# A hybrid attention and MoE block on one core: program order on TensorE from the output projection on, one weight load behind the last router scores, and a tail by token tiles

## The chip, the core and the metric

The kernel runs on one core of a Trainium2 chip. Its engines work side by side, each on its own queue of instructions in order: TensorE (PE, matmuls and transposes, with PEld for its weight loads), VectorE (DVE), ScalarE (ACT), GpSimd (POOL) and SyncE (SP), which here does nothing but issue transfers. They wait for each other by semaphores. The metric is the device time of one execution in microseconds (us), lower is better.

## What is computed

The block takes x of 512 tokens x 1024 columns. A condition vector gives shifts, scales and gates; two causal attention mixers run side by side, are gated and merged, and one output projection adds them to x. Then comes the part that this change is about:

```python
h = rms_norm(x, g_ffn_norm[l]) * (1.0 + scale_f) + shift_f
x = x + gate_f * moe_ffn(h, ...)
return rms_norm(x, g_final)

scores = sigmoid(xf @ w_router)                     # 512 x 64 experts
choice = scores + b_router
# the best 4 of 8 groups (by the sum of their top two), the top 6 experts in them
gate = take_along_axis(scores, expert_idx); gate = gate / gate.sum(-1) * 2.5
# every token goes to its 6 experts, rows sorted by expert
hb = silu(xb @ w_exp_gate[e]) * (xb @ w_exp_up[e])  # 1024 -> 256
routed += (hb @ w_exp_down[e]) * g[:, None]         # 256 -> 1024
shared = (silu(xf @ w_sh_gate) * (xf @ w_sh_up)) @ w_sh_down
```

There are 64 experts of 3 MB each in f32 and one shared expert of the same size. 512 x 6 rows are spread over them.

## The kernel before

All tokens stay on the core. Tokens are taken in four tiles of 128 (index i), the output projection also in four chunks of 256 columns (index c). A matmul is f32; where both factors are split in a high and a low part it is done in three passes (`mm3`, L155 to L158).

**From the output projection to the router.** `out_proj(i, c)` multiplies the merged mixers by a chunk of w_out and adds the gated result to `acc[:, i]`, the running x. When a token tile has all four chunks, `norm2(i)` (L902) normalises it: a sum of squares on ACT, a power on POOL, a scaled copy `h2p` on DVE, which is stored to `h2d` in DRAM for the later gathers and turned by eight PE transposes (`tp`) into `h2T`. `score(i)` (L919) multiplies `h2T` by the router weights into `lg` (L925), copies it to `lgT` on ACT and adds its halves by a second matmul (L929), and takes an exponential on ACT (`sc`). `route(i)` (L934) is a chain of small DVE operations that ends in `sel`, the 0/1 choice of experts for each token. `place(i)` (L981) counts with PE the rows ahead of each token (`pos`: `sel` of the earlier tiles by ones, of its own by a triangle) and makes addresses; `scatter(i)` (L998) writes six columns to a `table` in DRAM by indirect transfers of POOL. `shared_in` (L1013) is the first layer of the shared expert (`og` and `ou`, then `hs`), `shared_out` (L1028) the second (`so`, added to `acc` on DVE). From the counts of all four tiles (`cr`, `cc`) the kernel then ranks the experts by their load (`pm`, `sched`, L1050 to L1078) and finds those with more rows than their slots hold (`ob`, `om`, L1080 to L1115).

In this part a scheduler arranges PE's instructions of before by its own estimates; `follow` ties a few of them to others, and the table `SEQ` sets the order of the program's steps.

**The expert tiles.** Four experts are fixed ones, whose weights are loaded before the ranking is known; the others are loaded in order of rank, into six weight slots. The rows lie in 33 tiles of 128 rows, each with up to four experts. Per tile: `fetch` gathers 128 rows of `h2d` by an indirect POOL transfer into one of three buffers (two `xg` and the space of `hs`), `turn` transposes them (`tp`, `xT`), `first` multiplies by gate and up (`gu`), `hide` applies silu, `turn_hidden` transposes, `expert_out` multiplies by down (`y`), and `combine` adds the rows back to their tokens by matmuls with a one-hot `oht` (`o`, high and low part `yH`, `yL`). PE and SP are in an order written by hand (`manual_schedule`), and `ENTRY` is the order of the first transfers: g, u and d with a number are gate, up and down weights of a tile's first experts, s the pieces of the table, f a gather, e a reading of the ranking.

**The tail.** The last tile (number 32) multiplies in two groups of two experts; `seed` starts sums (`fo`) with `acc` by an identity matmul, y of the last tile is added to them, and when all four token tiles are done, ACT squares, POOL adds and takes powers, DVE scales, SP stores, one token tile after the other.

Of the kernel before, what the change touches and what calls it, by code (L numbers as in the profile page):

```python
# [10 lines left out]
F32 = mybir.dt.float32  # L11
# [6 lines left out]
ALU = mybir.AluOpType  # L18
# [21 lines left out]
HOLD = 0  # L40
HREST = (1, 2, 3)
FOL = 1
SEQ = (((2, 3), ()), ((3, 3), ["n0"]), ((2, 2), ()), ((3, 2), ["s0", "n1", "r0"]), ((2, 1), ()), ((3, 1), ["s1", "p0", "r1"]),
       ((2, 0), ()), ((3, 0), ["n2", "n3", "c0", "p1", "s2", "s3", "c1", "r2", "p2", "c2", "r3", "h0", "p3", "c3"]))
SEQ = [(p, [(t[0], int(t[1])) for t in todo]) for p, todo in SEQ]
PW = {0: 3, 1: 3}
CHM, SOB, SOC = 0, 2, 2
ENTRY = "e1 g1 s0 s1 f0 u1 s2 s3 f1 s4 s5 s6 s7 s8 d1 e3 g3 u3"
# [45 lines left out]
def build(ctx, tc, a, out, dbg=None):  # L94
# [593 lines left out]
    def load_expert(slot, e, parts=1, now=True):  # L688
# [126 lines left out]
    hs = keep.tile([128, 2, S], F32, name="hs")  # L815
    tb = keep.tile([128, TILES + 1, 2], I32, name="tb")
# [33 lines left out]
    scat = []  # L850

# [49 lines left out]
    def norm2(i):  # L901
        t = slice(i * 128, (i + 1) * 128)  # L902
        h2p = np2.tile([128, KD, 128], F32, name="h2p", bufs=2)
        A.activation(h2p.rearrange("p k f -> p (k f)"), acc[:, i], AF.Square, accum_out=st2[:, 0, i:i + 1])
# [4 lines left out]
        SP.dma_start(h2d[t], h2p.rearrange("p k f -> p (k f)"))  # L909
        for g in range(2):  # L910
            tp = tr_p.tile([128, S], F32, name="tp", tag="tr")
            for k in range(4):
                PE.transpose(tp[:, k * 128:(k + 1) * 128], h2p[:, g * 4 + k], ident)
# [6 lines left out]
    def score(i):  # L920
# [6 lines left out]
        A.copy(lgT, lg[:, :128])  # L927
        lg = mm_p.tile([128, S], F32, name="lg", tag="mm")
        PE.matmul(lg[:, :NE], lgT, pairs, start=True, stop=True)  # L929
        sc = rt.tile([128, NE], F32, name="sc", bufs=2)  # L930
        A.activation(sc, lg[:, :NE], AF.Exp, scale=-1.0)
        scores[i] = sc

    def route(i):  # L934
# [20 lines left out]
        chm = rt.tile([128, 8, 8], F32, name="chm")  # L955
        (V if CHM else G).memset(chm, NEG)
# [24 lines left out]
    def place(i):  # L981
        oh, ixf, pay = picks.pop(i)
        pos = mm_p.tile([128, S], F32, name="pos", tag="mm")
        for q in range(i):
            m = PE.matmul(pos[:, :NE], onesb, sel[:, q], start=(q == 0), stop=False)
            if q == 0 and FOL:
                follow(m, last[0])
        m = PE.matmul(pos[:, :NE], before, sel[:, i], start=(i == 0), stop=True)
        if FOL:
            follow(m, last[0])  # L990
# [22 lines left out]
    def shared_in(g, blocks=range(2)):  # L1013
        t = slice(g * 256, g * 256 + 256)
        for b in blocks:
            og = s_p.tile([128, S], F32, name="og", tag="s")
            ou = s_p.tile([128, S], F32, name="ou", tag="s")
            for j, o in ((0, og), (1, ou)):
                for k in range(KD):
                    m = PE.matmul(o[:, :256], wsg[:, j, k, b * 128:(b + 1) * 128], h2T[:, k, t],  # L1020
                                  start=(k == 0), stop=(k == KD - 1))
                    if k == 0 and g == 0 and 2 * b + j >= HOLD:
                        follow(m, last[0])
            A.activation(hs[:, b, t], og[:, :256], AF.Tanh, scale=0.5)
            V.scalar_tensor_tensor(hs[:, b, t], hs[:, b, t], 1.0, og[:, :256], op0=ALU.add, op1=ALU.mult)
            V.scalar_tensor_tensor(hs[:, b, t], hs[:, b, t], 0.5, ou[:, :256], op0=ALU.mult, op1=ALU.mult)

    def shared_out(rows):  # L1028
        for i in rows:
            for n in range(2):  # L1030
                o = mo_p.tile([128, S], F32, name="so", tag="y")
                for b in range(2):
                    PE.matmul(o, hs[:, b, i * 128:(i + 1) * 128], wsd[:, b, n * 512:(n + 1) * 512],
                              start=(b == 0), stop=(b == 1))
                c = slice(n * 512, n * 512 + 512)
                V.tensor_tensor(acc[:, i, c], acc[:, i, c], o, ALU.add)

    for c in range(4):
        for i in range(2):
            out_proj(i, c, chunks[c])  # L1040
# [17 lines left out]
    cr = mm_p.tile([128, S], F32, name="cr", tag="mm")  # L1058
    cc = mm_p.tile([128, S], F32, name="cc", tag="mm")
# [5 lines left out]
    rowk = rt.tile([128, NE], F32, name="rowk")  # L1065
# [3 lines left out]
    cmpk = rt.tile([NE, NE], F32, name="cmpk")  # L1069
    V.scalar_tensor_tensor(cmpk, rowk[0:NE], cnt[:, 1:2], ones[0:NE, 0:NE], op0=ALU.is_gt, op1=ALU.mult,  # L1070
                           accum_out=cnt[:, 2:3])
    ohr = rt.tile([NE, NE], F32, name="ohr")
    V.tensor_scalar(ohr, iota_e[0:NE], cnt[:, 2:3], None, op0=ALU.is_equal)
    pm = mm_p.tile([128, S], F32, name="pm", tag="mm")
# [3 lines left out]
    V.tensor_scalar(sched[:, 1], pm[0:1, :NE], float(STRIDE), None, op0=ALU.mult)  # L1078

# [396 lines left out]
```

## Time and profile before

| | |
|---|---|
| device time, 3 runs | 1071.81 us median (1068.25, 1071.81, 1071.98) |
| the profiled execution | 1072.04 us, of which its span holds 1070.3 |
| PE, busy share of the span | 1012.1 us, 95% |
| DVE, ACT, POOL | 580.1 us (54%), 316.4 us (30%), 160.8 us (15%) |
| DMA, mean over the span | 268 GB/s |

The span runs from the first instruction to the last event of the profiled execution, and 1.7 us of its time lie outside. A busy share is a mean over stages of very different kind, so the rows further down are taken stage by stage. PE's records overlap where matmuls are pipelined, and in one instruction of 512 columns f32 there are two records.

### The profile page before, as it was taken

The page shows a single profiled execution, that of the slowest core. Times are in us where ns is not written, and L with a number is a line of the kernel's source. Part 1 is how long each engine was busy: PE and PEld are TensorE (multiplying, and loading weights), DVE is VectorE, ACT ScalarE, POOL GpSimd, SP SyncE. Part 2 cuts the span into 40 slices and gives each one's busy share as a digit, 9 for nine tenths or more (in the row PEclk, how much of TensorE's full clock was granted, in tenths as well). Part 3 has the DMA queues.
Part 4 walks back from the last instruction along what each step waited for, and adds up shares of the span by engine and source line. Part 5 has one row for each costly group of instructions (what it writes and reads, how often), then busy time and mean ns, then how long its engine had stood idle before and what let it go on. Part 6 is the DMA issues. An engine that isn't in the chain of part 4 may idle for free.

```text
span 1070.3 us, 16307 instructions
## 1 busy us (share of the span) xinstructions
PE 1012.1 (95%) x5904; PEld 603.8 (56%) x5904; DVE 580.1 (54%) x1151; ACT 316.4 (30%) x694; POOL 160.8 (15%) x215
## 2 busy tenths in 40 slices
PE   7999999998989989977999999999999999999994
PEld 6678667776756669855434444444443444444431
DVE  3568576377668644863344445455444544544444
ACT  3445553233235432420122212212221221222203
POOL 2413001000121283055100000000000000000001
PEclk9999999999989999988999999999999999999997
DMA  8942105699461558443799998999999999999762
GB/s 242 299 140 61 52 0 163 196 285 279 140 197 30 175 190 301 144 170 98 282 393 409 417 404 328 383 414 415 390 380 371 381 410 413 350 411 408 281 212 79
DMA packets 104467, 286.11 MB, mean 267 GB/s; under 512 B 18241, under 2 KB 65049, under 8 KB 80322
## 3 DMA queue, kind: packets, MB, share of 16 engines
q1 hardware_dynamic: 97458, 270.33, 68.2%
q0 software_dynamic: 5648, 12.63, 3.1%
q10 hardware_dynamic: 1280, 2.10, 0.7%
q8 instruction: 47, 0.77, 0.3%
q14 instruction: 34, 0.28, 0.1%
HBM read 282.46 MB, written 4.66 MB: 268 GB/s over the span
## 4 chain that ended last, share of the span: by engine, by line
PE 78%; DVE 6%; DMA 5%; SPq 3%; POOL 2%; issue 2%; ACT 2%; another core or an unknown queue 1%; ACTq 0%; DVEq 0%; POOLq 0%
PE gu L1190 22%; PE y L1222 11%; PE o L157 6%; PE o L1246 6%; PE o L156 6%; PE o L158 6%; PE o L1247 6%; PE tp L1177 3%; PE sp L577 3%; PE oc L601 2%; PE tp L589 2%; DMA wm<-in_w_mod_dram 1%; PE og L1020 1%; PE ou L1020 1%
## 5 line engine op out<-in xcount | busy, mean ns | idle before, releaser
L1190 PE MATMUL gu<-gu,xT 128*32 128x512 f32 (+1 forms) x1664 | 241.8, 598 | 0.1
L1190 PEld LDWEIGHTS gu<-gu,xT 128*32 128x32 f32 (+1 forms) x1664 | 72.4, 118 | 153.3 <-issue 138.4
L1222 PE MATMUL y<-dn,hid 128*32 128x512 f32 (+1 forms) x832 | 121.6, 596 | 0.0
L1199 DVE TENSOR_TENSOR hid<-hid,gu 128x256 f32<-128x256 f32 x33 | 13.9, 420 | 171.5 <-ACT hid L1198 171.5
L1246 PE MATMUL o<-yH,oht 128*128 128x512 f32 x260 | 104.0, 400 | 0.7 <-DVE acc L1248 0.7
L1248 DVE TENSOR_TENSOR acc<-acc,o 128x512 f32<-128x512 f32 x140 | 93.4, 683 | 18.3 <-PE o L1247 18.2
L1247 PE MATMUL o<-yL,oht 128*128 128x512 f32 x260 | 101.7, 391 | 0.0
L157 PE MATMUL o<-hH,wL 128*128 128x512 f32 x208 | 82.6, 397 | 0.5 <-DVE wL L165 0.5
L156 PE MATMUL o<-hH,wH 128*128 128x512 f32 x208 | 82.5, 397 | 0.0
L158 PE MATMUL o<-hL,wH 128*128 128x512 f32 x208 | 81.7, 393 | 0.0
L162 ACT CAST yH<-ys 128x512 fp32r<-128x512 f32 (+1 forms) x68 | 41.1, 605 | 106.5 <-DVE ys L1226 106.5
L1222 PEld LDWEIGHTS y<-dn,hid 128*32 128x32 f32 (+1 forms) x832 | 32.6, 117 | 64.9 <-issue 54.7
L165 DVE TENSOR_TENSOR yL<-ys,yH 128x512 fp32r<-128x512 f32 (+1 forms) x68 | 45.9, 676 | 42.7 <-ACT yH L162 42.5
L1198 ACT ACTIVATE hid<-gu 128x256 f32<-128x256 f32 x33 | 12.7, 384 | 190.1 <-PE gu L1190 190.1
L1226 DVE SCALAR_TENSOR_TENSOR ys<-y,tb,gmb 128x512 f32<-128x512 f32 (+1 forms) x68 | 49.8, 734 | 31.3 <-PE y L1222 28.0
L1166 POOL DMA_INDIRECT xg<-h2d,tb x22 | 22.2, 1010 | 267.6 <-PE tp L1177 173.7
L1246 PEld LDWEIGHTS o<-yH,oht 128*128 128x128 f32 x260 | 48.8, 188 | 16.2 <-DVE acc L1248 3.1
L897 ACT ACTIVATE xT<-tp,ab 128x128 f32<-128x128 f32 x132 | 49.6, 456 | 24.0 <-PE tp L1177 15.0
L1247 PEld LDWEIGHTS o<-yL,oht 128*128 128x128 f32 x260 | 48.9, 188 | 10.2 <-DVE yL L165 0.8
L899 DVE TENSOR_SCALAR xT<-tp,ab 128x128 f32<-128x128 f32 x132 | 45.1, 403 | 4.5 <-PE tp L1177 2.1
L156 PEld LDWEIGHTS o<-hH,wH 128*128 128x128 f32 x208 | 39.1, 188 | 11.8 <-issue 1.9
L157 PEld LDWEIGHTS o<-hH,wL 128*128 128x128 f32 x208 | 39.1, 188 | 9.9 <-DVE wL L165 2.1
(380 smaller groups left out, 1674.9 us busy)
## 6 DMA issues: line engine op xcount, KB each, us to landing
gu<-in_w_exp_gate_dram SPq DMA_DIRECT2D x63, 1024.0 KB
gu<-in_w_exp_up_dram SPq DMA_DIRECT2D x63, 1024.0 KB
dn<-in_w_exp_down_dram SPq DMA_DIRECT2D x60, 1024.0 KB
w<-in_w_mod_dram SPq DMA_DIRECT2D x32, 512.0 KB
w<-in_w_in_dram SPq DMA_DIRECT2D x13, 1024.0 KB
wm<-in_w_mod_dram SPq DMA_DIRECT2D x16, 512.0 KB
wraw<-in_w_out_dram SPq DMA_DIRECT2D x12, 512.0 KB
dn<-in_w_exp_down_dram SPq DMA_DIRECT2D x8, 512.0 KB
```

What stands on the lines that cost most here:

```text
L156: PE.matmul(o, l[0], r[0], start=start, stop=False)
L157: PE.matmul(o, l[1], r[0], start=False, stop=False)
L158: return PE.matmul(o, l[0], r[1], start=False, stop=stop)
L165: return le.tensor_tensor(L, src, f(H), ALU.subtract)
L897: A.activation(out, src, AF.Identity, bias=ab2[:, 1, k:k + 1], scale=ab2[:, 0, k:k + 1])
L899: V.tensor_scalar(out, src, ab2[:, 0, k:k + 1], ab2[:, 1, k:k + 1], op0=ALU.mult, op1=ALU.add)
L1190: last[0] = PE.matmul(gu[lo:lo + n], xT[:, k, lo:lo + n], w[:, :, k], start=(k == 0), stop=(k == KD - 1))
L1222: last[0] = PE.matmul(y[lo:lo + m], hT[:, j, lo:lo + m], w[:, j, c], start=(j == 0), stop=(j == 1))
L1226: V.scalar_tensor_tensor(ys[:, b], y[:, b], f(tb[:, T, 1:2]), gfb[:, c][:, b], op0=ALU.mult, op1=ALU.mult)
L1246: m = PE.matmul(o, oht[:, i * 128:(i + 1) * 128], yH[:, c], start=(q == 0), stop=False)
L1247: PE.matmul(o, oht[:, i * 128:(i + 1) * 128], yL[:, c], start=False, stop=(q == len(state) - 1))
L1248: d = V.tensor_tensor(acc[:, i, c], acc[:, i, c], o, ALU.add)
```

## The change

From the output projection on PE now runs in program order (`order.__enter__()` ahead of the loop of the output projection, left ahead of the expert tiles), and the steps are written out one by one. `SEQ`, `HOLD`, `HREST`, `FOL` and the `follow` ties are gone. `norm2` is split in `norm_rows` and `norm_turn`, `score` in `score` and `score_sum`. `h2p` is written into the `xg` buffers, so POOL no longer clears them; the four `chm` buffers of the routes are cleared early. The shared expert's first layer is done in quarters and halves of a quarter between the router's steps, and its second layer for token tiles 0 to 2 moves ahead of the expert tiles; only tile 3 is left inside. The load of the fourth fixed expert first gets three ACT copies of one element from the last `sc`, so its three transfers stand behind the last exponential; the load of `gfb` and the `h2d` stores stand ahead of it. `ENTRY` has u1 and d1 ahead of the first pieces of the table.

In the tail the last tile multiplies in one group of four, the remaining state of tile 31 is combined half by `combine`, half straight into the sums (`part`), and each token tile is finished by itself (`add_last`, `store_last`). The sum of the squares moves from POOL to DVE, the scaling of one half from DVE to a product on DVE and one on ACT.

```diff
-ENTRY = "e1 g1 s0 s1 f0 u1 s2 s3 f1 s4 s5 s6 s7 s8 d1 e3 g3 u3"
+ENTRY = "e1 g1 u1 d1 s0 s1 f0 s2 s3 f1 s4 s5 s6 s7 s8 e3 g3 u3"
...
-    def load_expert(slot, e, parts=1, now=True):
+    def load_expert(slot, e, parts=1, now=True, after=None):
...
+        if after is not None:
+            for to in (gu[0:1, 0, 0, 0:1], gu[0:1, 1, 0, 0:1], dn[0:1, 0, 0:1]):
+                A.copy(to, after[0:1, 0:1])
...
-        h2p = np2.tile([128, KD, 128], F32, name="h2p", bufs=2)
+        h2p = xg[i % 2].rearrange("p (k f) -> p k f", k=KD)
...
+    def shared_in(g, b, j, ks=range(KD)):
...
+    order = tc.manual_schedule(engines={mybir.EngineType.PE})
+    order.__enter__()
     for c in range(4):
...
-    for (i, c), todo in SEQ:
-        out_proj(i, c, chunks[c])
-        for fn, j in todo:
-            {"n": norm2, "s": score, "c": scatter, "r": route, "p": place, "h": lambda j: shared_in(j // 2, [j % 2])}[fn](j)
+    lo, hi = range(0, 4), range(4, 8)
+    norm_rows(0)
+    norm_rows(1)
+    out_proj(2, 3, chunks[3])
...
+    norm_turn(3)
+    place(1)
+    score(2)
+    shared_in(0, 1, 0, lo)
+    score_sum(2)
+    score(3)
+    route(2)
+    scatter(1)
+    shared_in(0, 1, 0, hi)
...
+    WT[fixed[3]] = load_expert(4, slice(3, 4), after=score_sum(3))
     SP.dma_start(gfb, bc(modd[5 * D:6 * D]))
-    WT[fixed[3]] = load_expert(4, slice(3, 4))
+    shared_in(0, 1, 1)
+    place(2)
+    route(3)
+    scatter(2)
+    shared_out(0, mm_p, "mm")
+    shared_out(1, mm_p, "mm", [0])
+    place(3)
+    scatter(3)
...
+    shared_out(1, mm_p, "mm", [1])
+    shared_in(1, 0, 0, lo)
...
+    shared_in(1, 0, 0, hi)
+    shared_in(1, 0, 1)
+    shared_in(1, 1, 0)
...
+    shared_in(1, 1, 1)
+    shared_out(2, mm_p, "mm")
+    om = tr_p.tile([128, S], F32, name="om", tag="tr")
...
-    for j in range(2):
-        G.memset(xg[j], 0.0)
...
-    shared_out(range(SOB))
     turn_next(0, (0, 1))
-    shared_out(range(SOB, SOC))
+    shared_out(3, mo_p, "y")
     hidden = hide(*first([todo[0][0]], todo[0][1]))
-    shared_out(range(SOC, NT))
...
-    groups = [ents[i:i + TG] for i in range(0, len(ents), TG)]
-    hid = hide(*first(groups, xT))
+    hid = hide(*first([ents], xT))
+    combine(full, cols=halves[:1])
+    hT = turn_hidden(hid)
...
+    def part(i, states, c, start, stop):
+        t = slice(i * 128, (i + 1) * 128)
+        for q, (oht, yH, yL) in enumerate(states):
+            PE.matmul(sums[i], oht[:, t], yH[:, c], start=start and q == 0, stop=False)
+            PE.matmul(sums[i], oht[:, t], yL[:, c], start=False, stop=stop and q == len(states) - 1)
+
+    def seed(i):
+        tag, bufs = (("tr", 2), ("tr", 2), ("cb", 1), ("gu", GUB))[i]
+        sums.append(mo_p.tile([128, S], F32, name="fo", tag=tag, bufs=bufs))
+        PE.matmul(sums[i], ident, acc[:, i, halves[1]], start=True, stop=False)
+        part(i, full, halves[1], False, False)
+
+    seed(0)
     state = spread(toks.pop(T))
...
     expert_out(0, T, ents, hT, state, WIDE)
+    seed(1)
+    expert_out(1, T, ents, hT, state, WIDE)
+    seed(2)
+    seed(3)
...
+    def add_last(i):
+        combine([state], [i], ((("ht", 1), ("gu", GUB), ("ht", 1), ("y", 2))[i],), halves[:1])
+        square(i, 0, acc[:, i, halves[0]])
+        part(i, [state], halves[1], False, True)
+        square(i, 1, sums[i])
+        V.tensor_tensor(outs[i][:, halves[0]], acc[:, i, halves[0]], gfin[:, halves[0]], ALU.mult)
+        p = slice(i, i + 1)
+        V.scalar_tensor_tensor(fs[:, 0, p], fs[:, 0, p], EPS, fs[:, 1, p], op0=ALU.add, op1=ALU.add)
+        G.tensor_tensor(fs[:, 1, p], fs[:, 0, p], mh[:, 0:1], ALU.pow)
+
+    def store_last(i):
+        V.scalar_tensor_tensor(outs[i][:, halves[1]], sums[i], fs[:, 1, i:i + 1], gfin[:, halves[1]], op0=ALU.mult,
+                               op1=ALU.mult)
+        scaled = A.mul(outs[i][:, halves[0]], outs[i][:, halves[0]], fs[:, 1, i:i + 1])
+        for c in halves[::-1]:
+            SP.dma_start(outr[:, i, c], outs[i][:, c])
+        return scaled
...
+        add_last(i)
+        if i:
+            store_last(i - 1)
```

The order on PE around the last two router scores and the prefix counts (`pos`) of token tile 2, first before the change:

```order
L1020 MATMUL ou<-h2T,gu 128x256
L929 MATMUL lg<-pairs,lgT 128x64
L925 MATMUL lg<-h2T,wr 64x128 x8
L1020 MATMUL ou<-h2T,gu 128x256
L929 MATMUL lg<-pairs,lgT 128x64
L985 LDWEIGHTS onesb
L985 MATMUL pos<-sel,onesb 128x64
L985 LDWEIGHTS onesb
L985 MATMUL pos<-sel,onesb 128x64
L1020 MATMUL ou<-h2T,gu 128x256 x6
```

and with it (line numbers are those of the changed kernel):

```order
L937 MATMUL lg<-pairs,lgT 128x64
L1027 MATMUL ou<-h2T,gu 128x256 x8
L993 LDWEIGHTS onesb
L993 MATMUL pos<-sel,onesb 128x64
L993 LDWEIGHTS onesb
L993 MATMUL pos<-sel,onesb 128x64
L994 LDWEIGHTS before
L994 MATMUL pos<-sel,before 128x64
L1040 MATMUL so<-dn,hs 128x512 x6
L993 LDWEIGHTS onesb
L993 MATMUL pos<-sel,onesb 128x64
```

Whole blocks of the shared expert now stand between the last router sum and the prefix counts of tiles 2 and 3, and six matmuls of its second layer, which stood among the expert tiles, between those two.

The order on DVE in the same place with the change, behind token tile 2's addresses, up to a few rows ahead of tile 3's `sel`:

```order
L1041 TENSOR_TENSOR acc<-acc,so 128x512
L953 TENSOR_TENSOR gs<-g_4375 128x8
L957 TENSOR_TENSOR ahead<-gs 128x64
L958 TENSOR_TENSOR even<-gs 128x64
L959 COPY_PREDICATED ahead<-low_3468,even 128x64
L1041 TENSOR_TENSOR acc<-acc,so 128x512
L961 TENSOR_REDUCE gr<-ahead 128x8
L963 TENSOR_SCALAR kept<-gr 128x8
L965 COPY_PREDICATED chm_3497<-kept,ch 128x64
L969 MAX m_4396<-chm_3497 128x8
L970 MAX_INDEX ix<-m_4396,chm_3497 128x8
L1041 TENSOR_TENSOR acc<-acc,so 128x512
```

Three additions of the shared expert now stand inside the route of tile 3; before, they came after it, among the expert tiles.

On PE, the last tile's first product (`gu`), first before the change, with the sums `o` of tile 31:

```order
L1190 MATMUL gu<-gu,xT 32x512 x2
L1246 MATMUL o<-yH,oht 128x512
L1247 MATMUL o<-yL,oht 128x512
L1246 MATMUL o<-yH,oht 128x512
L1247 MATMUL o<-yL,oht 128x512
L1246 MATMUL o<-yH,oht 128x512
L1247 MATMUL o<-yL,oht 128x512
L1190 MATMUL gu<-gu,xT 32x512 x27
L1366 MATMUL fo<-acc,ident 128x512 x2
```

and with it:

```order
L1274 MATMUL y<-dn,hid 32x512 x16
L1242 MATMUL gu<-gu,xT 32x512 x32
L1298 MATMUL o<-yH,oht 128x512
L1299 MATMUL o<-yL,oht 128x512
```

The 32 instructions of `gu` now stand in one piece, and the sums follow it.

## Rows read from the trace of the kernel before

**Rows 1.** By stretch: busy us (x instructions) of PE, PEld, DVE, ACT, POOL; clock; DMA share; GB/s.

```profile
428.20:531.20 103.00, 87.25 (x518) 64.37 (x516) 57.55 (x212) 23.23 (x56) 32.20 (x39) 0.93 0.47 165
466.65:473.48 6.83, 4.13 (x12) 3.45 (x13) 0.75 (x4) 0.49 (x2) 4.58 (x5) 0.50 0.37 139
497.37:504.19 6.82, 5.61 (x17) 3.99 (x18) 1.93 (x11) 0.00 (x0) 2.21 (x3) 0.50 0.50 167
508.00:1022.00 514.00, 511.44 (x3249) 234.06 (x3251) 250.06 (x458) 114.32 (x261) 37.98 (x64) 1.00 0.95 381
1023.60:1054.60 31.00, 31.00 (x142) 11.10 (x138) 13.14 (x24) 4.74 (x12) 0.30 (x1) 1.00 0.32 106
```

**Rows 2.** Waits of PE, 428.2 to 545: waiting, releaser, us, times, longest.

```profile
PE lg L929 <- issue: 5.2, 1, 5.2
PE om L1106 <- DVE ov L1100: 4.7, 1, 4.7
PE pos L988 <- DVE sel L969: 2.4, 2, 1.8
PE ob L1096 <- DVE nbb L1094: 2.0, 1, 2.0
PE tp L1177 <- DMA hs<-h2d,tb: 1.5, 1, 1.5
```

**Rows 3.** Waits for an event of unknown source (remote), 428.2 to 545, same columns.

```profile
ACT lgT L927 <- remote: 6.3, 1, 6.3
...
DVE ovr L1097 <- remote: 5.3, 1, 5.3
```

**Rows 4.** Timeline of PE: start us, length us, instructions.

```profile
507.95 7.03 PE L1033 MATMUL so<-dn,hs 128*128 128x512 f32 x16
...
531.22 7.14 PE L1190 MATMUL gu<-gu,xT 128*32 128x512 f32 x64
```

**Rows 5.** Timeline of DVE in the router, last two token tiles.

```profile
476.20 0.78 DVE L969 TENSOR_REDUCE sel<-oh 128x64 bf16<-128x384 bf16 x1
...
482.68 0.81 DVE L969 TENSOR_REDUCE sel<-oh 128x64 bf16<-128x384 bf16 x1
```

**Rows 6.** Timeline of POOL: the last scatter and two gathers.

```profile
494.22 0.96 POOL L1002 DMA_INDIRECT table<-pay,adr  x1 [0.30 <-issue]
...
501.75 1.06 POOL L1166 DMA_INDIRECT xg<-h2d,tb  x1 [0.16 <-POOL xg L1134]
...
530.45 1.02 POOL L1166 DMA_INDIRECT hs<-h2d,tb  x1 [13.10 <-DMA tb<-table]
```

**Rows 7.** Timeline of SP: weight loads as they are issued.

```profile
452.98 0.33 SPq L704 DMA_DIRECT2D gu<-in_w_exp_gate_dram  x1
...
491.61 0.24 SPq L1289 DMA_DIRECT2D gu<-in_w_exp_gate_dram  x1
...
508.15 0.35 SPq L1289 DMA_DIRECT2D gu<-in_w_exp_gate_dram  x1
```

**Rows 8.** Groups of PE work after the last full tile, 1023.6 to 1055.

```profile
L1190 PE MATMUL gu<-gu,xT 128*32 128x512 f32 x64 | 13.7, 596 | 0.0
L1222 PE MATMUL y<-dn,hid 128*32 128x512 f32 x36 | 5.5, 598 | 0.0
...
L1366 PE MATMUL fo<-acc,ident 128*128 128x512 f32 x8 | 4.1, 619 | 0.0
```

**Rows 9.** Timeline of PE: the first of the last 14 multiplications.

```profile
1051.01 0.50 PE L1246 MATMUL o<-yH,oht 128*128 128x512 f32 x1
```

**Rows 10.** Groups of DVE work, 1023.6 to 1062.

```profile
L1248 DVE TENSOR_TENSOR acc<-acc,o 128x512 f32<-128x512 f32 x12 | 7.7, 682 | 2.4 <-PE o L1247 2.3
...
L1402 DVE SCALAR_TENSOR_TENSOR yo<-acc,fs,xg 128x512 f32<-128x512 f32 x2 | 1.5, 752 | 0.4 <-POOL fs L1398 0.4
```

**Rows 11.** Timeline of SP: the last stores.

```profile
1059.26 2.59 SPq L1404 DMA_DIRECT2D out_dram<-yo  x4
```

**Rows 12.** DMA rate in 40 slices of 1.25 us, 1015 to 1065.

```profile
GB/s 262 239 338 351 403 411 297 72 200 252 241 306 329 383 382 372 66 2 0 0 0 0 0 0 0 0 0 0 0 0 0 0 13 167 325 347 349 313 184 0
```

More of the change, by code (lines that the diff above doesn't have):

```diff
@@ L850, in build @@
     scat = []
+    chms = [rt.tile([128, 8, 8], F32, name=f"chm{i}") for i in range(NT)]
+    for i in range(NT):
+        G.memset(chms[i], NEG)
     np2 = pool("np2", 1, stack=nst)
@@ L982, in place @@
         oh, ixf, pay = picks.pop(i)
-        pos = mm_p.tile([128, S], F32, name="pos", tag="mm")
+        pos = o_p.tile([128, S], F32, name="pos", tag="oc")
         for q in range(i):
[L985 to L990, printed above, removed]
+            PE.matmul(pos[:, :NE], onesb, sel[:, q], start=(q == 0), stop=False)
+        PE.matmul(pos[:, :NE], before, sel[:, i], start=(i == 0), stop=True)
         ohs = r_([128, 6, NE], F32, "ohs")
@@ L1011, in build @@
     wsg, wsd = shared
-    def shared_in(g, blocks=range(2)):
+    halves = [slice(0, 512), slice(512, 1024)]
+    shared_ps = {}
+    def shared_in(g, b, j, ks=range(KD)):
         t = slice(g * 256, g * 256 + 256)
[L1015 to L1036, printed above, removed]
+        if ks[0] == 0:
+            shared_ps[j] = s_p.tile([128, S], F32, name="ou" if j else "og", tag="s")
@@ new lines, in shared_in @@
+        o = shared_ps[j]
+        for k in ks:
+            PE.matmul(o[:, :256], wsg[:, j, k, b * 128:(b + 1) * 128], h2T[:, k, t], start=(k == 0), stop=(k == KD - 1))
+        if ks[-1] < KD - 1:
+            return
+        if j:
+            V.scalar_tensor_tensor(hs[:, b, t], hs[:, b, t], 0.5, o[:, :256], op0=ALU.mult, op1=ALU.mult)
+        else:
+            A.activation(hs[:, b, t], o[:, :256], AF.Tanh, scale=0.5)
+            V.scalar_tensor_tensor(hs[:, b, t], hs[:, b, t], 1.0, o[:, :256], op0=ALU.add, op1=ALU.mult)
@@ L1038, in build, with shared_out @@
+    def shared_out(i, pool, tag, ns=range(2)):
+        for c in (halves[n] for n in ns):
+            o = pool.tile([128, S], F32, name="so", tag=tag)
+            for b in range(2):
+                PE.matmul(o, hs[:, b, i * 128:(i + 1) * 128], wsd[:, b, c], start=(b == 0), stop=(b == 1))
+            V.tensor_tensor(acc[:, i, c], acc[:, i, c], o, ALU.add)
+    order = tc.manual_schedule(engines={mybir.EngineType.PE})
+    order.__enter__()
     for c in range(4):
@@ L1399, in build @@
-    for i in range(NT):
-        for n in NORD:
-            src = sums[i] if n else acc[:, i, halves[0]]
-            V.scalar_tensor_tensor(outs[i][:, halves[n]], src, fs[:, 1, i:i + 1], gfin[:, halves[n]], op0=ALU.mult,
-                                   op1=ALU.mult)
-            SP.dma_start(outr[:, i, halves[n]], outs[i][:, halves[n]])
-    for i in range(NT):
-        follow(A.copy(acc[:, i, halves[1]], sums[i]), sq)
+        return A.activation(outs[i][:, halves[1]], src, AF.Square, scale=1.0 / 32.0, accum_out=fs[:, n, i:i + 1])
@@ L1408, in finish_more @@
+    order.__exit__(None, None, None)
+    for i in range(NT):
+        follow(A.copy(acc[:, i, halves[1]], sums[i]), scaled)
     def finish_more(state):
```

103 lines of the change are left out of this document (45 added, 58 removed).

## The prediction

> **What bounds the kernel now.** I read the stages first. From 428.2 to 531.2 us, the stretch from the last output projections to the first matmul of the second expert tile, PE is busy for 87.25 of 103.00 us, so 15.75 us of that stage are idle although it has work for all of it [rows 1]. In the 514 us of expert tiles that follow it is busy for 511.44, at full clock [rows 1]: that stage is bound by PE and only the moment at which it starts can move. From 1023.6 to 1054.6 PE is busy throughout, but with work of another shape, and after 1054.6 it has nothing left while DVE, ACT, POOL and SP finish the output; the last store leaves SP at 1059.26 + 2.59 = 1061.85 [rows 11]. Second, PE's waits say who ends the idle 15.75 us. The two longest are 5.2 us ahead of the router's sum (lg) and 4.7 us ahead of the overflow table (om); 2.4 us are spent on the prefix counts (pos), which wait for DVE's selection, and 2.0 us on ob [rows 2]. The view names no engine for the first, and DVE for the second. But the engines behind them waited in turn for an event that the profile cannot place: ACT's copy of lgT for 6.3 us and DVE's copy of ob for 5.3 us, each directly behind a PE result that is long done in the records [rows 3]. So two signals from PE came about 5 us late, and each time PE then stood still. [...] It works 4.13 and 5.61 us in these stretches, half of which, 2.1 + 2.8 = 4.9 us, is the price of the lower clock.
>
> **The change before the expert tiles.** It adds and removes next to no arithmetic there; it changes who may pass whom. What is left is 87.25 − 4.9 = 82.4 us of PE work at full clock (the shared expert's output is all in it, 7.03 us for each two token tiles [rows 4], one block before the first expert tile and one behind it). To this I add the waits that the new order leaves.
>
> The one I can size is place(3). DVE delivers sel of token tile 3 6.5 us after that of tile 2 today (476.20 to 482.68 [rows 5]). In the new DVE order three sums acc += so stand between the two; at the 0.68 us of a DVE addition of this size [rows 10] they make it 6.5 + 2.0 = 8.5 us. PE has place(2) and three halves of shared_out in between, 6 instructions of 7.03 / 8 = 0.88 us each [rows 4], together 5.3, and some 0.6 for the small prefix matmuls. So PE waits 8.5 − 5.9 = 2.6 us. For the three other places where PE follows DVE or ACT closely (score_sum(0), place(2), pm) I take 0.4 each, an estimate between nothing and the 1.8 us of the longer pos wait of today [rows 2], nearer to nothing because matmuls of 2 us and more stand ahead of each. ob and om have 3 to 6 us of shared-expert work ahead of them in the new order, more than the 2.0 that ob lacks, so I count nothing; if that cover were gone, they would cost 2.0 and, with an on-time signal, about 1. The clock fell after idle times of 5.2 and 4.7 us [rows 1, 2]; 2.6 us is about half of these, so I leave between nothing and 2 us for it and take 1.
>
> First gu of the second tile: 428.2 + 82.4 + 2.6 + 1.2 + 1 = 515.4, against 531.22 [rows 4]: **−15.8 us**. The third tile's gather, which PE waits for today for 1.5 us [rows 2], is issued at 530.45 since its buffer hs is read by the late shared_out; in the new order only row tile 3 is left there, so it can go 10 us before it is needed or more: **−1.5 us**. Together −17.3, bounds −22 (no wait left, no lower clock) and −11 (each small wait at 1.8 us, 2 us for the clock, ob uncovered).
>
> Does something else hold the tiles up? Today's sched is out on SP at 491.61, where the first scheduled weights start [rows 7]; the scatters on POOL end at 494.22 + 0.96, and the first gather goes at 501.75 [rows 6], 6.6 us later, the last of it behind POOL's clearing of xg, which the change drops (I count 0.7). Ahead of route(3) the 5.2 us of waiting and 2.1 of low clock go, and 2.0 of additions and some 0.7 of waits come, so scatters and sched are 4.6 us earlier; the first gather then goes at about 496.5, and has to be there when PE turns the first tile, two transposes (1 us each), 1.8 us of so and 7.1 us of gu before 515.4, so at about 503.5. Its landing has a lower bound of its 1.06 us on POOL; the upper one is the hs gather under full load, 530.45 until PE goes on at 531.22 + 7.14 + 1.5 = 539.9, so 9.4 us. At 496.5 the three loads of the first scheduled expert (issued at about 487, 3.1 MB at some 400 GB/s, 8 us) are through, so I take 3 us: in time by 4. By the upper end PE would wait 2.4 us.
> [...]
>
> The weights: the loads g3 and u3 are issued at 508.15 today [rows 7], 23 us before their first use at 531.22. They go when the shared expert's input weights are done with, about 501 in the new order, 14 us before use; 2.1 MB at 381 GB/s [rows 1] need 5.5. Over the tiles the DMA moves 381 GB/s [rows 1] and single slices reach 411 [rows 12], so 514 us of transfers fit in 514 × 381 / 411 = 476 us. Tiles that end 17 us earlier leave 497 for them.
>
> **The tail.** gu of the last tile takes 13.7 us as two groups of two experts; a tile in one group of four takes 7.14 [rows 4, 8]: −6.6 us of PE. The same 8 + 8 sums of tile 31, 4 ident seeds, 16 last sums and y stay, 31.0 − 13.7 = 17.3 us at most; in unbroken runs they need less (ident 4.1 us for 8 records, y 5.5 for 36 [rows 8]). I put 16.5, so PE ends 23.6 us after 1023.6 instead of 31.0. The halves of the last down weights arrive until about 1036 (slices to 66 GB/s [rows 12]); y(1) begins some 14 us after 1023.6, 1037.6 on this scale: no wait, by 1.6 us. Behind PE DVE becomes the limit: for each token tile an addition 0.68, a product of the same size 0.68, a small sum 0.15 and the scaled half 0.75 [rows 10], 2.26 us, for four 9.0. Today the last 14 multiplications run from 1051.01 to 1054.6 [rows 9], 3.6 us; 16 take 4.1. So DVE starts 23.6 − 4.1 + 0.5 = 20.0 after 1023.6, ends at 29.0, and with a square root's wait of 0.5 and a store's issue of 0.6 the last store is out at 30.1, against 1061.85 − 1023.6 = 38.25: **−8.2 us**. Bounds −6 (PE saves only the 6.6, and y(1) waits) and −10 (DVE's work hidden but for the last tile).
>
> **Sum.** 1072.04 (the profiled run, 0.2 us over the median) − 17.3 − 8.2 = 1046.5; I say 1046.
>
> **Rivals.**
> (B) The late signals come again. What ties them to the load of the fourth fixed expert is that this load starts at 452.98 [rows 7] and that lgT was late while DMA was full; but om's was late with the scheduled loads on their way. The moved load now leaves at about 468, while place(2) and the sums of so hand their results to DVE. If one is late by 5 us, DVE stands with route(3) queued behind it: 5.2 − 2.6 already counted, + 2.1 to 2.8 for the clock, so 4.7 to 5.4 us, and 8 if it hits a second place. 1051 to 1054. For it: both bursts of loads ahead of the tiles had such an event. Against it: the load is one short burst of 3.1 MB, and a late result costs only where DVE or ACT has nothing else to do. If the events are tied to something else and both return, 5.2 + 4.7 − 2.6 + 4.9 = 12 us are lost, 1058.
> [...]
> (C) Gathers or weights come late after all: every expert tile is then later by the same, up to the full 15.8. 1055 to 1063. Against it are the margins of 4 and 7 us.
> (D) Slower than before. PE in strict order passes no wait. It has eight places there at which it needs a result of DVE or ACT (four sums, four prefix counts), besides pm, ob and om. Where each is missed, PE stands for it in full, while today the scheduler's order has other matmuls between them. The price of one miss is at most the 6.5 us of a route on DVE; the tail and the hs gather give 9.7, so it turns slower when the idle time rises from 15.75 to over 25 with the low clock as today, at four full misses; five give 428.2 + 82.4 + 32.5 + 4.9 = 548.0 for the second tile, 16.8 later, and 1079. The order of DVE speaks against it, where routes alternate with PE's blocks of 3 us and more.
> (E) The tail saves only half, since ACT (two squares and a product per tile) or late weights hold it: 1050.
>
> **Chances.** The forecast (1041 to 1049) 0.50, B 0.29 (0.05 of it for both events), E 0.06, C 0.07, D 0.04, better than 1041 0.04. The range from 1038 to 1059 leaves out D and part of C. Below 0.5% (5.4 us) a measurement of this kernel can't be told from no change: faster 0.92 (all but D and a rest), same 0.04, slower 0.04.
>
> **What would show it.** PE's waits for lg by "issue" and for om are gone, pos has one wait of about 2.6 us, and no 6.8 us stretch at 0.50; the second tile's first gu is at about 515; PE is near 100% from there; gu of the last tile takes 7 us in one piece, and the last stores are out 30 us after tile 31's y. Wrong would be: a remote event of some 5 us again, a wait of tp for a gather or of gu for weights in the first tiles, y(1) waiting for DMA, or a start of the tiles later than 520.

## The result, and the profile after

| | kernel before | changed kernel |
|---|---|---|
| executions compared | 1066.6 to 1071.98 us, median 1070.03 | 1053.89 and 1056.05 us |
| ratio, 95% interval | | 0.9852 (0.9824 to 0.9880) |
| the profiled execution (its span) | 1072.04 us (1070.3) | 1053.89 us (1052.2) |

The changed kernel is 1.5% faster. Two of its four executions in this comparison took 5659 us and are left out of the ratio; they did not come again in 6 later executions of it or in 51 of its variants, and no trace of one exists.

PE's timeline, start and length, shows gu of the first two tiles and the last tile's gu behind y of tile 31:

```profile
514.17 7.07 PE L1242 MATMUL gu<-gu,xT 128*32 128x512 f32 x64
...
524.17 7.07 PE L1242 MATMUL gu<-gu,xT 128*32 128x512 f32 x64
```

```profile
1009.78 3.64 PE L1274 MATMUL y<-dn,hid 128*32 128x512 f32 x32
1013.23 7.05 PE L1242 MATMUL gu<-gu,xT 128*32 128x512 f32 x64
```

The second tile's gu comes at 524.17, 7.05 us earlier than in [rows 4]; I had put it at 515.4. y of tile 31 ends 10.2 us earlier. So 3.2 us more come between the two. The gather of the third tile no longer stops PE, 1.5 us [rows 2], and the trace of before has, near the end of the tiles, one stretch at half the clock that the changed one lacks, 1.7 us (by stretch, columns as in [rows 1]):

```profile
999.10:1002.50 3.40, 3.40 (x17) 0.79 (x20) 0.28 (x1) 0.62 (x2) 0.00 (x0) 0.50 0.72 272
```

The last store, on SP:

```profile
1040.56 2.93 SPq L1450 DMA_DIRECT2D out_dram<-yo  x4
```

Its issue ends at 1043.49, 30.1 us after y of tile 31 ends (1013.42); before it was 38.25 [rows 11]. So the 18.15 us between the two profiled executions are 7.05 ahead of the tiles, 3.2 in them and 8.15 in the tail, less 0.26 behind the last store.

What PE waits for up to the third tile, columns as in [rows 2]:

```profile
PE pos L994 <- DVE sel L977: 2.6, 2, 2.4
PE lg L937 <- issue: 2.3, 1, 2.3
PE pos L994 <- DVE oh L974: 2.3, 1, 2.3
PE tp L1257 <- DVE hid L1251: 1.5, 1, 1.5
PE tp L1229 <- DMA xg<-h2d,tb: 1.2, 1, 1.2
```

Of the two long waits of [rows 2] the one for lg is down from 5.2 to 2.3 us and that for om is gone. The wait of 2.3 for `oh` is pos of tile 3, which I had at 2.6. New are 2.35 us at pos of tile 2, 1.5 at the hidden tile of the first expert tile and 1.2 at the first gather. And late signals as in [rows 3] are still there, waits that end by an event which the profile can't place. Both are now on ACT (the trace of before has a third one, 3.2 us ahead of ACT's `sc` behind the late lgT):

```profile
ACT lgT L932 <- remote: 4.7, 1, 4.7
ACT hs L1033 <- remote: 4.7, 1, 4.7
```

By stretch, columns as in [rows 1], first the one that holds both, then the two at half the clock:

```profile
461.00:476.00 15.00, 12.15 (x76) 9.81 (x74) 6.60 (x31) 3.30 (x12) 11.56 (x12) 0.89 0.03 2
470.50:473.90 3.40, 3.40 (x9) 2.69 (x9) 0.00 (x0) 0.00 (x0) 2.48 (x4) 0.50 0.02 1
487.60:491.00 3.40, 3.40 (x8) 2.01 (x7) 2.60 (x13) 0.00 (x0) 2.06 (x3) 0.51 0.02 1
```

In the stretch with the late signals DMA is idle: a share of 0.03, 2 GB/s. The fourth expert's load does not start before 475.14:

```profile
475.14 0.33 SPq L700 DMA_DIRECT2D gu<-in_w_exp_gate_dram  x1
...
501.75 7.58 SPq L1198 DMA_DIRECT2D tb<-table  x9
```

ACT goes on at 469.45 (lgT) and at 474.40 (hs), so both signals had come, late, before this load began. The low clock in the stretch of [rows 1] is down from two times 6.8 us to two times 3.4 us, in which PE is busy throughout, a price of 1.7 us each. Ahead of that stretch the trace of before has one more, which no forecast counted: from 401.8 to 405.2 us the clock is 0.50 and PE busy throughout, so 1.7 us, and the changed kernel lacks it. On POOL the last scatter and the first gather, 10 us later than I had put it:

```profile
495.40 0.96 POOL L1006 DMA_INDIRECT table<-pay,adr  x1 [0.30 <-issue]
506.34 1.06 POOL L1218 DMA_INDIRECT xg<-h2d,tb  x1 [9.98 <-DMA tb<-table]
```

### The profile page after: what moved, and what is told of

It is laid out like the page before. It is cut to its first block, busy times and chain, and to the rows that moved or that the text cites. A ratio compares the mean times of both kernels' runs of the same rounds, so it can differ in the third digit from the quotient of the medians.

```text
span 1052.2 us, 16301 instructions
## 1 busy us (share of the span) xinstructions
PE 1001.2 (95%) x5904; PEld 602.8 (57%) x5904; DVE 575.1 (55%) x1151; ACT 320.5 (30%) x701; POOL 156.1 (15%) x209
## 4 chain that ended last, share of the span: by engine, by line
PE 80%; DVE 6%; DMA 5%; SPq 3%; issue 2%; POOL 2%; ACT 1%; POOLq 0%; ACTq 0%; DVEq 0%
PE gu L1242 22%; PE y L1274 11%; PE o L150 6%; PE o L149 6%; PE o L151 6%; PE o L1298 6%; PE o L1299 5%; PE tp L1229 3%; PE sp L570 3%; PE oc L594 2%; PE tp L582 2%; DMA wm<-in_w_mod_dram 1%; PE og L1027 1%; PE tp L1257 1%; DMA w<-in_w_mod_dram 1%
## 5 line engine op out<-in xcount | busy, mean ns | idle before, releaser
L1242 PE MATMUL gu<-gu,xT 128*32 128x512 f32 (+1 forms) x1664 | 233.4, 594 | 0.0
L1242 PEld LDWEIGHTS gu<-gu,xT 128*32 128x32 f32 (+1 forms) x1664 | 69.1, 117 | 150.7 <-issue 137.0
L1300 DVE TENSOR_TENSOR acc<-acc,o 128x512 f32<-128x512 f32 x136 | 91.0, 686 | 17.4 <-PE o L1299 17.4
L151 PE MATMUL o<-hL,wH 128*128 128x512 f32 x208 | 82.4, 396 | 0.0
L900 DVE TENSOR_SCALAR xT<-tp,ab 128x128 f32<-128x128 f32 x132 | 45.2, 405 | 10.2 <-ACT xT L898 7.4
```

What stands on the lines that cost most here:

```text
L151: return PE.matmul(o, l[0], r[1], start=False, stop=stop)
L900: V.tensor_scalar(out, src, ab2[:, 0, k:k + 1], ab2[:, 1, k:k + 1], op0=ALU.mult, op1=ALU.add)
L1242: last[0] = PE.matmul(gu[lo:lo + n], xT[:, k, lo:lo + n], w[:, :, k], start=(k == 0), stop=(k == KD - 1))
L1300: d = V.tensor_tensor(acc[:, i, c], acc[:, i, c], o, ALU.add)
```

## The experiments

They ran in three groups of four, each group on a chip of its own with the kernel before beside it. A number that compares them is the time from the first matmul of the output projection to gu of the second tile, in the profiled execution ("stage" below). It is 135.4 us in the kernel before (395.81 to 531.22) and 126.0 in the changed one (398.14 to 524.17). The chip of that first comparison is not on record. Each stage is one execution, and it holds whatever low clock fell into it: the 1.7 us at about 402 us of the kernel before are also in e5, e10 and (1.6 us, at 400) e8, in either order.

| kernel | median us | kernel before beside it, us | ratio (95%) | stage us | remote waits |
|---|---|---|---|---|---|
| e1_tail | 1044.27 | 1050.77 | 0.9940 (0.9920 to 0.9960) | 117.8 | none |
| e2_nowait | 1048.00 | 1050.77 | 0.9960 (0.9940 to 0.9980) | 121.3 | none |
| e3_scatter | 1046.80, one | 1050.77 | | 121.9 | none |
| e4_sums | 1048.32 | 1050.77 | 0.9975 (0.9957 to 0.9993) | 121.8 | none |
| e5_after | 1045.27 | 1052.19 | 0.9934 (0.9920 to 0.9948) | 124.1 | none |
| e6_tail2 | 1044.73 | 1052.19 | 0.9916 (0.9894 to 0.9937) | 119.1 | none |
| e7_entry | 1045.64 | 1052.19 | 0.9948 (0.9929 to 0.9967) | 118.1 | none |
| e8_fix | 1040.80 | 1052.19 | 0.9891 (0.9876 to 0.9906) | 116.0 | none |
| e9_fixnowait | 1057.43 | 1071.72 | 0.9875 (0.9829 to 0.9922) | 123.6 | 7.7, 4.6 |
| e10_fixoldtail | 1063.60 | 1071.72 | 0.9931 (0.9907 to 0.9954) | 132.4 | 7.1, 4.0, 3.1, 1.0 |
| e11_entryalone | 1065.36 | 1071.72 | 0.9947 (0.9918 to 0.9976) | 135.5 | 10.3, 8.4, 2.7 |
| e12_so3 | 1055.57 | 1071.72 | 0.9864 (0.9818 to 0.9910) | 127.1 | 9.2, 3.2 |

**e1_tail.** The kernel before with the changed tail, from `late_dn` to `finish_more`, and nothing else.

```diff
-    combine(full)
...
-    groups = [ents[i:i + TG] for i in range(0, len(ents), TG)]
-    hid = hide(*first(groups, xT))
+    hid = hide(*first([ents], xT))
+    combine(full, cols=halves[:1])
...
+    for i in range(NT):
+        add_last(i)
+        if i:
+            store_last(i - 1)
```

> The kernel before with the new tail alone (last tile in one group of four, token tiles finished one by one). From the end of tile 31's second product to the end of the span the changed kernel takes 1052.2 - 1013.2 = 39.0 us, the kernel before 46.7. If the tail is a part of its own, this kernel is 7.7 us faster than before (ratio 0.993), with PE's stretch from 428 to 531 us as before. If instead the tail only gains because the tiles start earlier (its down weights land in time), y of the second half waits for DMA and the gain is under 4 us.

It is 6.5 us faster by the medians, with y of tile 31 at 998.36 for 3.64 us and the last store, on SP, out at 1032.03:

```profile
1029.11 2.92 SPq L1401 DMA_DIRECT2D out_dram<-yo  x4
```

That is 30.0 us after y of tile 31, as in the changed kernel: the tail is a part of its own. But the trace holds more. This is the old order of PE on another chip, and there PE's waits are

```profile
PE pos L988 <- DVE sel L969: 1.5, 1, 1.5
PE lg L929 <- ACT lgT L927: 0.7, 2, 0.4
...
PE tp L913 <- DVE h2p L907: 0.6, 1, 0.6
```

with gu of the second tile at

```profile
512.66 7.14 PE L1190 MATMUL gu<-gu,xT 128*32 128x512 f32 x64
```

No wait by "issue", none for om, no remote one. The kernel before itself takes 1050.77 us there, 19 us less than in the comparison above. The two waits on which my forecast for the part ahead of the tiles rests belong to one series of executions, not to the order of the instructions alone.

**e2_nowait.** The load of the fourth fixed expert behind the h2d stores, without the copies that tie it to the last score.

```diff
-    WT[fixed[3]] = load_expert(4, slice(3, 4), after=score_sum(3))
+    score_sum(3)
+    WT[fixed[3]] = load_expert(4, slice(3, 4))
```

> The changed kernel with the fourth fixed expert's load put behind the h2d stores on SP, but not made to wait for the last score. Theory 1, late signals go with queued loads: ACT's copy lgT and the exponential wait 5 us or more for PE again as in the kernel before, the low clock lasts 6.8 us, and it is 3 to 6 us slower than the changed kernel. Theory 2, the late signals have nothing to do with the load: they stay at about 4.7 us each as in the changed kernel, where DMA is idle in that stretch, and the time is within 2 us of the changed kernel.

There is no late signal, with the load early. On this chip there is none with it late either, so the run does not separate the two theories; e12 does. Its stage is 3.5 us longer than that of the tail alone beside it.

**e3_scatter.** The program's calls of `scatter(0)` to `scatter(2)` behind `place(3)`.

```diff
-    scatter(0)
     norm_turn(3)
...
     place(3)
+    scatter(0)
+    scatter(1)
+    scatter(2)
     scatter(3)
```

> The changed kernel with all 24 scatters of POOL behind place(3), so that POOL is idle while the last two router scores run. This is for the trace, not the time: the table is complete some 15 us later, so the first gather and with it the tiles come late by 10 to 18 us. Theory 2a, the late signals come with the scatters: ACT's copy lgT and the tanh wait under 1 us, PE's idle time ahead of the last router sum (2.3 us) and of pos of tile 2 (2.4 us) goes. Theory 2b, they come from PE or ACT itself (instruction supply, order): both waits stay at 4 to 5 us.

It tested nothing: the change puts only PE and, later, SP in program order, and POOL's own order stayed, the first scatter at

```profile
457.94 1.16 POOL L1006 DMA_INDIRECT table<-pay,adr  x1 [4.21 <-DVE adr L1000]
```

It stands as one more trace of the changed order without late signals: a stage of 121.9 us.

**e4_sums.** The shared expert's second layer for tiles 0 and 1 behind place(3).

```diff
-    shared_out(0, mm_p, "mm")
-    shared_out(1, mm_p, "mm", [0])
+    shared_in(1, 0, 0)
+    shared_in(1, 0, 1, lo)
     place(3)
     scatter(3)
...
-    shared_out(1, mm_p, "mm", [1])
-    shared_in(1, 0, 0, lo)
+    shared_in(1, 0, 1, hi)
+    shared_out(0, mm_p, "mm")
...
-    shared_in(1, 0, 0, hi)
-    shared_in(1, 0, 1)
+    shared_out(1, mm_p, "mm")
     shared_in(1, 1, 0)
```

> The changed kernel with the shared expert's second layer for tiles 0 and 1 behind place(3) and quarters of its first layer in its place, so that no addition of 512 columns stands in the route of tile 3 on DVE. If the additions make sel of tile 3 late, PE's wait for it falls from 2.3 us to under 1 and the schedule of the experts is out 2 us earlier; the time falls by up to 2 us. If DVE's route itself is the length that counts, the wait stays.

```profile
PE tp L1228 <- DMA xg<-h2d,tb: 4.4, 1, 4.4
PE pos L994 <- DVE sel L977: 1.8, 2, 1.5
```

The longer pos wait falls from 2.3 to 1.5, not under 1: the additions are a part of it, the route itself the rest. DVE starts `sel` of tile 3 7.0 us after that of tile 2 here (467.75 and 474.79), against 8.3 to 8.4 with the additions between. PE is earlier at the first tile and waits there for the gather, 4.4 us. The stage stays (121.8): the wait has moved.

**e5_after and e6_tail2.** The changed kernel as it is and the tail alone, side by side.

> The changed kernel as it is, beside the tail alone. In the kernels run so far PE shows no late signal, and there the stretch from the shared expert's first matmul (452 us) to gu of the second tile takes 60.8 us in the old order (the tail alone) and 65.2 to 65.7 in the new one. Theory U: without late signals the new order loses 4 to 5 us and the tail gains 6 to 7, so this kernel is 1 to 4 us faster than before (ratio 0.996 to 0.999), and slower than the tail alone by 4 us. Theory L: the new order gains on any execution, so it is at least 5 us faster than the tail alone (ratio 0.989 or less).

> The kernel before with the new tail alone, a second time, to stand beside the changed kernel. Theory U: ratio 0.994 again, 4 us faster than the changed kernel. Theory L: slower than the changed kernel by 5 us or more.

Theory L falls: the changed kernel is 0.5 us slower than the tail alone by the medians, not 5 faster. Theory U's 4 us are not there by the medians either; the profiled executions differ by 5.0 us in the stage, but that of the changed kernel was the longest of its six (1050.94), and 1.7 of the 5.0 are the low clock at 402 us. What the order loses there, in its waits (PE):

```profile
PE tp L1229 <- DMA xg<-h2d,tb: 3.7, 1, 3.7
PE pos L994 <- DVE sel L977: 2.6, 2, 2.3
PE tp L1257 <- DVE hid L1251: 1.5, 1, 1.5
```

**e7_entry.** The changed kernel with the old `ENTRY`.

```diff
-ENTRY = "e1 g1 u1 d1 s0 s1 f0 s2 s3 f1 s4 s5 s6 s7 s8 e3 g3 u3"
+ENTRY = "e1 g1 s0 s1 f0 u1 s2 s3 f1 s4 s5 s6 s7 s8 d1 e3 g3 u3"
```

> The changed kernel with the old order of the first transfers: the first pieces of the table go ahead of u1 and d1. In the new order the first piece leaves SP 4.8 us after the last scatter, in the old one 1.2 us, and PE waits 1.8 to 4.4 us for the first gather. If the 2 MB of u1 and d1 ahead of the table are the cause, the first gather is issued 3 us earlier or more, PE's wait for it is gone, and the time falls by 1.5 to 2 us against the changed kernel. If the scatters' own landing is the cause, the gap of 4.8 us stays and nothing changes.

SP and POOL in e5_after, with 3 MB of loads ahead of the table (the 483.80 row is the first, u1 and d1 follow within 1.1 us):

```profile
483.80 0.36 SPq L1341 DMA_DIRECT2D gu<-in_w_exp_gate_dram  x1
...
495.47 7.59 SPq L1198 DMA_DIRECT2D tb<-table  x9
```

```profile
489.00 0.96 POOL L1006 DMA_INDIRECT table<-pay,adr  x1 [0.30 <-issue]
499.01 1.06 POOL L1218 DMA_INDIRECT xg<-h2d,tb  x1 [9.05 <-PE om L1166]
```

and in e7_entry:

```profile
489.90 1.49 SPq L1198 DMA_DIRECT2D tb<-table  x2
```

```profile
486.20 0.95 POOL L1006 DMA_INDIRECT table<-pay,adr  x1 [0.30 <-issue]
493.64 1.06 POOL L1218 DMA_INDIRECT xg<-h2d,tb  x1 [6.49 <-issue]
```

The first piece of the table leaves SP 5.5 us after the last scatter ends on POOL (489.96 to 495.47) with the loads ahead, 2.75 without u1 and d1 (487.15 to 489.90), and the gather goes 5.4 us earlier; the other 2.8 of these are the scatters' own earlier end. PE's wait for it is gone and the second gu comes at

```profile
512.21 7.08 PE L1242 MATMUL gu<-gu,xT 128*32 128x512 f32 x64
```

so the stage is 118.1 us. The median, though, is that of e5_after (1045.64 against 1045.27; e7's executions reach from 1041.89 to 1048.65, and the profiled one was the shortest). In this pair of traces the gap shrinks with the loads moved, and PE's wait goes; that it saves 2 us of the time is not shown.

**e8_fix.** e4's order, the old `ENTRY`, and the shared expert's last sum behind the first gu.

```diff
     turn_next(0, (0, 1))
-    shared_out(3, mo_p, "y")
     hidden = hide(*first([todo[0][0]], todo[0][1]))
+    shared_out(3, mo_p, "y")
```

> The changed kernel with three parts of the new order taken back or moved: the table ahead of u1 and d1, the second layer of the shared expert's tiles 0 and 1 behind place(3) instead of ahead of it, and that of tile 3 behind gu of the first tile, where it covers silu. Waits that should go: first gather (2 to 4 us), the product of the hidden tile (1.5), pos of tile 3 (2.3 to under 1.5). Theory U: second tile's gu 4 to 5 us earlier than in the changed kernel, and with the tail 0.992 to 0.994 of before. If the waits only move to the next place, it gains under 2 us on the changed kernel.

```profile
PE pos L994 <- DVE sel L977: 1.8, 2, 1.5
PE tp L1228 <- DMA xg<-h2d,tb: 1.0, 1, 1.0
```

```profile
510.64 7.61 PE L1241 MATMUL gu<-gu,xT 128*32 128x512 f32 x64
```

The silu wait is gone, the gather's is 1.0, pos has 1.8 in two. It is the shortest stage of all (116.0) and the best kernel: 1040.63 to 1041.06 in four executions, 4.5 us less than the changed kernel by the medians, and the intervals of the two do not touch. That of the tail alone beside it does (e6, 0.9894 to 0.9937), so that the repaired order is worth anything here beyond the tail is not shown.

**e9_fixnowait.** e8 with the load as in e2. The next four ran on a chip on which the kernel before takes 1071.72 us, as in the first comparison.

> The repaired order (table ahead of u1 and d1, sums behind place(3), last sum behind the first gu) without the wait of the fourth fixed expert's load for the last score: on SP it goes right behind the h2d stores. Theory 1, the load disturbs the router: the tanh and score steps on ACT come late or the low clock lasts longer, and it is 2 us or more slower than the repaired order (0.991 or more). Theory 2, the wait buys nothing on an undisturbed execution: the same time within 1 us (0.988 to 0.990), and no wait in PE's list grows.

Here the late signals are back. SP and ACT in e9_fixnowait, whose load is issued at 449.40, and ACT in e12_so3, whose load waits for the last score:

```profile
449.40 0.33 SPq L700 DMA_DIRECT2D gu<-in_w_exp_gate_dram  x1
```

```profile
ACT lgT L932 <- remote: 7.7, 1, 7.7
...
ACT hs L1033 <- remote: 4.6, 1, 4.6
```

```profile
ACT lgT L932 <- remote: 9.2, 1, 9.2
...
ACT hs L1033 <- remote: 3.2, 1, 3.2
```

In e9 the load runs until about 465 us, 4.8 us before lgT starts at 469.80 (from 465 to 470 DMA moves 7 GB/s); in e12 it has not begun, its issue comes at 477.07, behind both. ACT waits 8 to 9 us for lgT either way and 3 to 5 at the next step. Of the four runs on this chip the one without the wait has the second-best ratio and the best stage. Theory 1 falls as a cause of the late signals. What the wait costs or saves in time stays open, since e8 did not run on this chip.

**e10_fixoldtail.** e8 with the old tail.

> The repaired order with the old tail, so the part ahead of the tiles alone. Theory U, the two parts add up: 0.9891 / 0.9925 = 0.9966 of before, some 3 to 4 us, of which PE's stretch up to gu of the second tile shows 1.5 to 2. Rival: the repaired order brings nothing by itself (0.999 to 1.001), and its time with the new tail was the tail's on a good chip.

7 us by the ratio, twice what I expected, on a chip with late signals, of which it had its share:

```profile
ACT lgT L932 <- remote: 7.1, 1, 7.1
...
DVE acc L1041 <- remote: 3.1, 1, 3.1
```

Its stage is 3.0 us shorter than that of the kernel before in the first comparison (135.4). It is not the rival's zero. Whether it adds up with the tail to 0.9891 can't be told, since that is from another chip; on this chip 0.9931 times the 0.9947 of e11 (the tail with the changed `ENTRY`) is 0.9878, and e9, which has both parts without the load's wait, has 0.9875.

**e11_entryalone.** The tail alone with the changed `ENTRY`.

> The tail alone with the changed kernel's order of the first transfers, so u1 and d1 ahead of the table, in the old order of PE. If these 2 MB hold up the table, the first piece leaves SP 5 us after the last scatter instead of 1.2 to 2, the first gather goes 3 us later, and PE waits for it 1 to 3 us: 1 to 3 us slower than the tail alone (0.994 to 0.996). If the wait seen in the changed kernel is due to its order on PE, nothing changes (0.992).

Inconclusive. PE waits 7.3 us for lg and 5.2 for ob, behind late signals, longer than for any gather, and no wait for the first gather is left to see:

```profile
ACT hs L1024 <- remote: 10.3, 1, 10.3
...
ACT lgT L927 <- remote: 8.4, 1, 8.4
```

**e12_so3.** The changed kernel with the old `ENTRY` and the last sum behind the first gu.

> The changed kernel with the table ahead of u1 and d1 and the shared expert's last sum behind the first gu; the sums of tiles 0 and 1 stay ahead of place(3). If the uncovered silu cost 1.5 us, PE's wait of the hidden tile's transposes is gone and gu of the second tile comes 59 us after the shared expert's first matmul instead of 60.5; pos of tile 3 still waits 2.3. Time 1 to 2 us less than with the transfers' order alone (0.990 to 0.993). If the wait moves to the gather of the third tile, which now goes behind that sum, the time stays.

```profile
PE lg L937 <- ACT lgT L932: 7.5, 1, 7.5
PE pos L994 <- DVE sel L977: 2.5, 2, 2.3
```

The silu wait is gone and pos of tile 3 stays at 2.3, as expected; the 7.5 us ahead of them are the late lgT.

## Why the prediction was right, and where not

The time lies in the range, and the sign is right; the change is about 60% of the size that I gave (15.8 to 18 us against 25.8). That it is not less is in part luck: the comparison fell into a series of executions with late signals. Beside the kernel before of 1052.19 us the same change gives 6.9 us (e5), about a quarter of the forecast.

**The tail: right, by its own steps.** gu in one piece 7.05 us (7.14 forecast), the last store 30.1 us after y of tile 31 (30.1 forecast), y of the second half not held by its weights. e1 shows the same 30 us alone. Two small misses cancel: PE ends 22.4 us after y of tile 31 (23.6 forecast, 1035.83), and DVE takes 10.0 us from its first addition to the last scaled half (9.0 forecast, 1032.69 to 1042.65).

**The part ahead of the tiles: the mechanism was wrong.** The step that failed is the sum "82.4 us of PE work at full clock" plus "the waits that the new order leaves", where both late signals and all of the low clock were taken as gone with the old order. The stretches of the 4.9 us in that sum are the two of [rows 1] with a granted clock of 0.50, 466.65 to 473.48 and 497.37 to 504.19; PE works 4.13 and 5.61 us in them, and half of that is the price. In the changed kernel two waits of 4.7 us remain and cost PE 2.3 (lg) and 2.35 us (pos of tile 2, since DVE stands behind ACT's late tanh), and there are 3.4 us of price for the low clock instead of 1. Measured are 7.05 us and the 1.5 of the hs gather, 8.6 together, outside the bounds of 11 to 22 (the terms named for the lower one add up to 10.1). Ahead of 428.2 us, which the sum takes as fixed, two things nearly cancel: the changed kernel reaches the output projection 2.3 us later, and the kernel before has the 1.7 us of low clock at 401.8.

So the likeliest case did not come, but the second, B, "1051 to 1054": 1053.89. The number is B's, its cause is not: that the load makes these signals late is refuted (after and e12 have them before it begins, and e2 has none with it early). That the old order does is refuted by e1 and e6, where it has none. What makes them late stays open. They show in every trace of two series, the first comparison and the last four runs, each time at the last token tile's lgT, in five of the six also at ACT's next step, in some at a later step of ACT or DVE, whatever stood around, and in none of the eight other traces. Chip and time of running change together here, so the chip as such is not shown to be the cause. No run tests the scatters, which run at that time (e3). One lead is in the traces: lgT of the last tile is the 544th of ACT's instructions both in before and in after, and in both an 8 KB packet of an instruction queue (q14) moves while ACT waits for it (before: at 467.54, lgT at 469.03; after: at 467.91, lgT at 469.45). In e12 one moves at 466.92, lgT at 472.81. Ahead of the second late step no such packet moves in before and after (none from 469 to 475), so whether ACT waits for instructions is not shown.

With late signals the new order gains: e9 and e12 against e11, all with the new tail on one chip, have 0.9875 and 0.9864 against 0.9947 (e11 alone has u1 and d1 ahead of the table, so not all of that need be the order on PE), and the interval of e12 does not touch that of e11 (e9's does, just). In the profiled executions PE waits 4.7 us for om and 2.0 for ob in the old order (before) or 5.2 for ob (e11), and for neither in the new one (after, e9, e10, e12); the stage is 135.4 and 135.5 us against 126.0, 123.6, 132.4 and 127.1. Without late signals it is no shorter: 117.8 and 119.1 in the old order with the new tail, 121.3 to 124.1 in the new one, and 118.1 and 116.0 in the new one with the old `ENTRY` (e7, e8).

**Steps that were right.** pos of tile 3 waits 2.3 us (2.6), behind a `sel` 8.3 us after that of tile 2 (8.5). The hs gather's 1.5 us are gone, no tile waits for weights, and the gain at the tiles' start is kept to their end.

**Steps that were mis-sized or missed.** The first gather: I had it issued at 496.5 and in time by 4 us; it went at 506.34 and PE waited 1.2, in e4 4.4. I had taken today's distance from the last scatter to the gather over, 6.6 us less the memset; but with u1 and d1 ahead of the table it is 10.0 us (496.36 to 506.34), and the scatters were 1.2 us later than before instead of 4.6 earlier. (The 503.5 of that working should be 504.5 by its own terms, and it leaves out the second tile's transposes.) Its landing was as I took it: issued at 506.34, PE goes on at 509.71, 3.4 us, with no load under way (DMA at 1 GB/s from 505.00 to 506.30). Beside loads the traces show both ends of my range. In e7 the first gather, issued at 493.64 with u1 just issued (DMA share 0.78), landed after 3.7 us, and one issued at 499.77 (DMA share 0.97) after 9.6. So two gathers took over 9 us at a DMA share of 0.97, this one and that of hs in the kernel before (9.4 us, 530.45 to 539.90, DMA share 0.97), but behind which transfers they stood no row shows. The silu of the first tile: the change moved 7 us of sums from behind it, the block "behind" the first expert tile, and I priced that cover at nothing; uncovered, it cost 1.5 us, and e8 and e12 got it back.

Rival D, strict order that turns slower, has its sign in the runs without late signals: there PE's stage is 3 to 5 us longer than in the old order. The tail's 6.5 to 7.5 us outweigh it.

## What to carry to other kernels

Before a stall is priced as a gain, see whether another execution of the same kernel on another chip has it: here 10 of the 15.75 idle us and the low clock behind them belong to one kind of series. When work is moved out from behind an operation, list what it covered there, the silu of a first tile (1.5 us here) or the landing of a gather (1.2 us of PE's wait in after, 4.4 in e4), and price that cover. A transfer that others wait for (the table) should not be put behind megabytes that nobody needs for 30 us: in the traces its first piece left SP 5.5 us after the last scatter's end behind them (e5) and 2.75 us without them (e7), though the time of e7 does not show the gain.

## What the runs showed of the hardware that was not expected

The same program takes 1049 to 1055 us on two chips and 1063 to 1078 on a third, and the stage of the old order with the new tail, 117.8 to 119.1 us, becomes 135.5 there (with the changed `ENTRY`). In the six traces with late signals ACT's copy of the last lgT starts 3.9 to 9.1 us after the end of PE's product, with DMA at 2 GB/s (after) as well as at 349 (before, 462.70 to 469.40).

The first read of what POOL scattered leaves SP 4.8 to 5.5 us after the last scatter's end in five traces with 3 MB of loads issued ahead (after, e2 to e5), and 1.2 to 2.75 us after it in six with 1 MB (before, e1, e6 to e9). In e12 it is 4.35 us with 1 MB, so the loads ahead are not all of it.
